# Latent attention: keys and queries stored by head, one score product per block of queries, rotary part padded to 128 rows

## The chip, the cores and the metric

The program runs on one core of one Trainium2 chip. The metric is the time in microseconds (us) that the device takes for one execution; lower is better. A core has a matrix engine (PE in the profile; PEld is its loading of the stationary operand), a vector engine (DVE), a scalar engine (ACT), GpSimd (POOL) and a queue engine (SP) that only issues transfers here.

## The reference

A two-layer decoder trunk over 512 tokens of width 1024. Every layer is a half-step feed-forward network, a token mixer, a second half-step feed-forward network and a gated embedding. Layer 0's mixer is a gated one; layer 1's mixer is the latent attention that the change touches:

```python
def mla_mixer(h, positions, w_in, q_a_norm, kv_a_norm, w_q_b, w_kv_b, q_norm, k_norm, w_out):
    z = h @ w_in
    c_q, c_kv, k_rope = jnp.split(z, [Q_LORA, Q_LORA + KV_LORA], axis=-1)
    q = (rms_norm(c_q, q_a_norm) @ w_q_b).reshape(bsz, seq, C_HEADS, C_QK)      # 8 heads, 128 + 64
    kv = (rms_norm(c_kv, kv_a_norm) @ w_kv_b).reshape(bsz, seq, C_HEADS, C_NOPE + C_V)
    k_nope, v = jnp.split(kv, [C_NOPE], axis=-1)
    k = jnp.concatenate([k_nope, broadcast(k_rope)], axis=-1)
    q, k = rms_norm(q, q_norm), rms_norm(k, k_norm)
    # the last 64 features of q and k are rotated by the position
    ...
    def attend(args):                       # a block of 128 queries
        s = jnp.einsum('bhqd,bhkd->bhqk', qb, k) * ATTN_SCALE
        s = jnp.where(key_pos <= q_pos, s, NEG_BIG)
        return jnp.einsum('bhqk,bhkd->bhqd', jax.nn.softmax(s), v)
    return out @ w_out
```

A score is thus a sum over 192 features: 128 plain ones of the head and 64 rotary ones.

## The kernel before, in words

All activations stand as tiles of 128 features by 512 tokens. Weight products are made from weights and inputs each cut into a high and a low part of a reduced float32 kind (`mm3`, lines 125 to 129; `mm3t`, lines 163 to 167): three products for each, with up to 512 columns. Inside the attention the operands are whole float32, and there a product that is not a transpose shows as two records in the trace.

`odd` (line 860) is the attention. `latent` makes the compressed keys, values and queries. `keys(c)` and `values(c)` each work on four heads, and leave keys by tokens; `turn_keys(c)` turns them to features by tokens. `queries(c)` works on two heads and is a generator: four steps make the queries of a block of 128 tokens each, then comes the rotation on POOL, then `turn` (line 1084) for each of the four blocks of tokens: two transposes for the heads' plain features, with a copy by ACT, and one for the two heads' rotary features, which lie in rows 0 to 63 and 64 to 127 of one tile, with a copy by DVE.

`score(h, i)` (line 1017) makes the scores of a head for the i-th block of 128 queries. As keys lie by blocks of tokens, it runs over the i + 1 blocks of keys and issues for each a product over 128 rows (line 1025) and a product over the head's 64 rotary rows (line 1026), each with 128 columns. Over 8 heads and 4 blocks these are 80 products of either kind. Then DVE adds the mask and takes the maximum, ACT takes the exponential, and DVE divides.

The order is that of the loop at line 1060 over 32 pairs (h, i), from which a scheduler makes a fixed order for each engine. A step transposes the scores (line 1067), has ACT copy them, takes one step of `fill` (the queries of the other heads) or of the output projection, issues the scores three pairs ahead, and multiplies by the values (line 1075). Scores and transposed scores take turns in four PSUM tiles named `pb`, so the scores of a pair go into the tile that the scores two pairs earlier leave when their exponential is done.

Of the kernel before, what the change touches and what calls it, by code (L numbers as in the profile page):

```python
# [29 lines left out]
# columns of the constants' array  # L30
C_ID, C_BASE, C_LEV, C_NEG, C_ONE, C_INV, C_END = 0, 128, 256, 576, 704, 705, 737
LEVELS = (4, 8, 16, 32, 64)
# columns of the small parameters' array
# [4 lines left out]
def turn_parts(shift):  # L38
    """2**shift / (2 pi), less whole turns, in three parts: of 12 bits after the point, of the next 12, and the rest;
    each over 2**shift"""  # L40
    from fractions import Fraction
    two_pi = Fraction(62831853071795864769252867665590057683943388, 10 ** 43)
    unit = Fraction(2) ** shift
    rest = unit / two_pi
    rest -= round(rest)
    parts = []
    for bits in (12, 24):
        part = Fraction(round(rest * 2 ** bits), 2 ** bits)
        parts.append(float(part / unit))
        rest -= part  # L50
    return parts + [float(rest / unit)]


class Net:
# [14 lines left out]
    def share(self, *engines):  # L69
        """who takes the weights' low parts, in turn"""  # L70
        self.cutters = cycle(engines or (self.nc.vector,))

# [24 lines left out]
    def weights(self, src, total, unit, keep=False, step=CW, eng=None):  # L97
        """(hi, lo, n) for each unit columns of src"""
# [14 lines left out]
    def cut(self, h, l, src, eng=None):  # L113
        """src (float32) into h + l"""
# [3 lines left out]
    def cut_scaled(self, h, l, src, g):  # L118
        """src * g, g a column, into h + l"""
# [11 lines left out]
    def feat(self, src, x):  # L131
        """[P features, T] = W.T x; src [P, nk * P], a column of tiles"""
# [9 lines left out]
    def feats(self, ws, x, pss, t):  # L142
        """several at a time, for the tokens t; a step is an input's tile. ws: for each the pieces of the weights"""
# [9 lines left out]
    def tok_steps(self, src, x, width, pss):  # L153
        """into pss, TB tiles [P tokens, width], x.T W; src [P, nk * width], k-major; a step is a k"""
# [14 lines left out]
    def tok_blocks(self, src, x, width):  # L169
        """for each block of tokens [P tokens, width] = x.T W, with all of W held"""  # L170
# [16 lines left out]
    def rsqrt_steps(self, v, n):  # L187
# [8 lines left out]
        # with h = v y^2: y (15 - 10 h + 3 h^2) / 8, here without a factor of 3 / 8  # L196
# [6 lines left out]
        # y (3 - v y^2) / 2, with that factor  # L203
# [6 lines left out]
    def sums(self, sqs):  # L210
        """[P tokens, TB * len(sqs)] sums over partitions of [P, T] tiles"""
# [7 lines left out]
    def spread(self, r, c0):  # L219
        """PSUM [P, T], each partition with the tokens' values r[:, c0:c0 + TB]"""  # L220
# [6 lines left out]
    def norm_of(self, acc, d):  # L227
        """the tokens' 1 / rms, a column per block"""
# [5 lines left out]
    def along(self, r):  # L234
        """the same along the free axis, in each partition"""
# [14 lines left out]
    def done(self, k, t=slice(0, T), later=False):  # L250
        """x[k] is final for the tokens t: its part of the next stage's input"""
# [7 lines left out]
    def add_sq(self, acc, src, first, last):  # L259
        """acc, the squares' sum"""  # L260
# [10 lines left out]
    def ffn(self, i, f, g_next, embedding=False, tail=None, first=None):  # L271
        """tail: what is left of the stage before, for the second half of the tokens, in steps"""
# [58 lines left out]
    def project_out(self, w, mixed, g_next, early):  # L331
        """mixed: a list that grows; the first three outputs' sums over its first early tiles run ahead, a step each"""
# [25 lines left out]
    def ple(self, i, g_next):  # L358
        """By halves of the tokens, so that the norm of one runs beside the products of the other; returns the steps
        left for the second half. Two tiles of outputs lie side by side."""  # L360
# [49 lines left out]
        def finish(half, m, pps):  # L410
            """the last two outputs, one by one; the squares' sum then is in the first half of its tile"""
# [72 lines left out]
        # the other half begins with the weights that the first ended with  # L484
# [10 lines left out]
    def even(self, j, g_next):  # L495
# [3 lines left out]
        # lower bounds: softmax over one row, its running sum less its first  # L499
# [117 lines left out]
        def advance(us):  # L617
            """the recurrence's steps, in turn by heads, beside so much of the projections"""
# [53 lines left out]
    def hgrn_head(self, f, k, q, v, h, outs):  # L672
        """Decay products instead of exponentials of sums of logarithms: every factor of a pair (s, t) is a product
        of gates after s up to t, cut at a block's boundary, but in blocks of four, which are cut in their middle,
        where a factor may be the inverse of two gates (no gate is under F_MIN)."""
# [36 lines left out]
        # inside blocks of four  # L712
# [8 lines left out]
        # from a block's left half to its right half; each pair belongs to one level  # L721
        tt = t4
        for li, b in enumerate(LEVELS):
# [12 lines left out]
            # blocks twice as long  # L736
# [10 lines left out]
        # the state before each block of 128 tokens but the first  # L747
# [33 lines left out]
    def rope_tables(self):  # L781
        """cos and sin of the positions' angles, [P tokens, TB * 32]"""
# [13 lines left out]
        # in turns: the angle is cut into three parts of 12 bits and a rest, whose products with a turn's parts are exact  # L796
        part, cnt, frac, turns, low = (self.small() for _ in range(5))

        def whole(out, src, scale, unit):
            """src * scale, rounded to multiples of the unit"""  # L800
# [27 lines left out]
        # cos(a) = sin(pi / 2 - |a|)  # L828
# [4 lines left out]
        # with the rope parts' gains: first half and second half  # L833
# [10 lines left out]
    def rotate(self, V, out, src, nm, nh):  # L844
        """out, src [P, TB, nh, 64]"""
# [14 lines left out]
    def odd(self, j, g_next):  # L860
# [7 lines left out]
        def latent(m0, n, col):  # L868
            """gained by features, and the squares' sum"""
# [11 lines left out]
        # the rotary key, by features and then by tokens  # L881
# [9 lines left out]
        # the factors of both norms, by tokens, and their squares: latent keys and values, latent queries  # L891
# [31 lines left out]
        # keys by four heads: [features, head, token] for each block of tokens  # L923
        kT, krT = [[None] * 2 for _ in range(TB)], [[None] * 2 for _ in range(TB)]
# [33 lines left out]
        def turn_keys(c):  # L958
            kn, krs = ks.pop(c)
            for tb in range(TB):  # L960
                if c == 0:
                    t = self.big()
                    krT[tb] = [t[:, :256], t[:, 256:]]
                kT[tb][c] = self.big()
                self.turn(kT[tb][c], krT[tb][c], kn[tb], krs[tb], par[:, S_KN:S_KN + 1])
# [9 lines left out]
        def queries(c):  # L975
            """of two heads; their factors of the norms go to the softmax"""
# [22 lines left out]
            qT = [[None, None] for _ in range(TB)]  # L999
            two = [self.big() for _ in range(2)]  # L1000
            rope = self.big()
            for tb in range(TB):
                qT[tb][0] = two[tb // 2][:, tb % 2 * 256:tb % 2 * 256 + 256]
                qT[tb][1] = rope[:, tb * P:(tb + 1) * P]
                self.turn(*qT[tb], qn[tb], qo[:, tb * P:(tb + 1) * P], par[:, S_QN:S_QN + 1])
                rq = next(steps, rq)
                if tb == 1:
                    yield True
# [5 lines left out]
            heads[c] = qT, rq, nq  # L1014

        # a head's scores for a block of queries, and the softmax
        def score(h, i):
            c4, e4, e2 = h // 4, h % 4, h % 2
            pair, po = e4 // 2, 64 * e2
            qT, rq, nq = heads[h // 2]  # L1020
            n = (i + 1) * P
            ps = self.pb()
            for jj in range(i + 1):
                u = slice(jj * P, (jj + 1) * P)
# [215 lines left out]
```

## Time and profile before

| what | value |
|---|---|
| median of 3 runs | 2084.04 us (2083.5 to 2087.65) |
| span of the profiled execution | 2083.4 us |
| PE busy | 2034.7 us, 98% of the span |
| DVE, ACT, POOL busy | 1062.0, 772.9, 163.1 us |
| mean granted clock of PE | 0.990 |

The page gives the profiled execution's span and no other time of it; 2083.4 us is 0.64 us below the median of the runs. A row of the timeline that ends in "x2" stands for two instructions in a row, and the length that it shows goes from the start of the first to the end of the last; as instructions overlap, the pace is read from the distance between starts.

### The profile page before, as it was taken

The numbers are of one execution on the slowest core, as the hardware profiler recorded it, in microseconds if no ns is written. First come the engines' busy times: TensorE is split into PE (matmuls) and PEld (weight loads), VectorE is DVE, ScalarE is ACT, GpSimd is POOL, SyncE is SP. The second block draws the span as 40 slices with busy tenths as digits, with TensorE's granted clock in tenths as the row PEclk, the third lists the DMA queues.
The fourth block names the chain that finished last, engine by engine and source line by source line (L and its number), as shares of the span: only waits on it lengthen the run. The fifth ranks groups of instructions, "written<-read, shape, count | busy, mean of one in ns | idle before, by whom it ended". The sixth has DMA issues, their size and how long they took to land.

```text
span 2083.4 us, 25822 instructions
## 1 busy us (share of the span) xinstructions
PE 2034.7 (98%) x9924; PEld 1708.6 (82%) x9924; DVE 1062.0 (51%) x2021; ACT 772.9 (37%) x1364; POOL 163.1 (8%) x152
## 2 busy tenths in 40 slices
PE   8999999999999999999899999999999999999997
PEld 6888888778888888889888888887778888888896
DVE  6444444676555444445874443445664554444456
ACT  5333333223343333334543333335543443333344
POOL 1000000210010000000210000003310100000002
PEclk9999999999999999999999999999999999999998
DMA  5333233222223232333422333332100232323333
GB/s 176 92 101 97 91 95 102 76 86 61 72 81 111 92 102 92 102 102 119 137 82 92 101 94 91 103 92 71 36 31 21 81 110 93 101 92 102 102 119 107
DMA packets 59324, 193.28 MB, mean 93 GB/s; under 512 B 6720, under 2 KB 9280, under 8 KB 59200
## 3 DMA queue, kind: packets, MB, share of 16 engines
q1 hardware_dynamic: 59200, 191.62, 29.7%
q8 instruction: 78, 1.28, 0.3%
q14 instruction: 46, 0.38, 0.1%
HBM read 189.50 MB, written 2.10 MB: 92 GB/s over the span
## 4 chain that ended last, share of the span: by engine, by line
PE 92%; DVE 5%; ACT 1%; DMA 1%; issue 0%; POOL 0%; SPq 0%; ACTq 0%; DVEq 0%; POOLq 0%
PE ps L127 26%; PE ps L129 26%; PE ps L128 26%; PE pb L1026 2%; PE pb L1025 1%; PE ps L165 1%; PE ps L166 1%; PE ps L167 1%; PE ps L1075 1%; DVE wl L116 1%; PE pb L730 1%; DVE big L693 1%; PE pb L129 1%; PE pb L128 1%; PE pb L127 1%; DMA raw<-in_w_gu 1%
## 5 line engine op out<-in xcount | busy, mean ns | idle before, releaser
L127 PE MATMUL ps<-big,wh 128*128 128x512 f32 (+1 forms) x2528 | 967.7, 383 | 9.1 <-ACT wh L115 5.9
L129 PE MATMUL ps<-big,wl 128*128 128x512 f32 (+1 forms) x2528 | 965.8, 382 | 8.3 <-DVE wl L116 8.2
L128 PE MATMUL ps<-big,wh 128*128 128x512 f32 (+1 forms) x2528 | 964.9, 382 | 0.0
L115 ACT CAST wh<-raw 128x512 fp32r<-128x512 f32 (+1 forms) x709 | 430.4, 609 | 1032.9 <-PE ps L128 857.0
L116 DVE TENSOR_TENSOR wl<-raw,wh 128x512 fp32r<-128x512 f32 (+1 forms) x677 | 486.0, 720 | 566.1 <-ACT wh L115 545.8
L129 PEld LDWEIGHTS ps<-big,wl 128*128 128x128 f32 x2528 | 475.8, 188 | 102.0 <-DVE wl L116 10.0
L127 PEld LDWEIGHTS ps<-big,wh 128*128 128x128 f32 x2528 | 475.8, 188 | 100.4 <-ACT wh L115 5.9
L128 PEld LDWEIGHTS ps<-big,wh 128*128 128x128 f32 x2528 | 476.1, 188 | 91.5 <-DVE big L116 0.2
L268 POOL TENSOR_TENSOR acc<-acc,tmp 128x512 f32<-128x512 f32 (+1 forms) x54 | 67.5, 1250 | 1587.9 <-ACT tmp L266 1587.0
L282 DVE TENSOR_TENSOR tmp<-ps,tmp 128x512 f32<-128x512 f32 x84 | 58.0, 691 | 117.4 <-PE ps L129 115.7
L280 DVE TENSOR_TENSOR tmp<-ps,rb 128x512 f32<-128x512 f32 x84 | 58.0, 691 | 115.7 <-PE ps L129 115.7
L121 DVE SCALAR_TENSOR_TENSOR big<-x,par,big 128x512 fp32r<-128x512 f32 (+1 forms) x72 | 58.2, 813 | 35.0 <-ACT big L120 34.5
L116 DVE TENSOR_TENSOR big<-tmp,big 128x512 fp32r<-128x512 f32 x96 | 67.7, 707 | 7.9 <-ACT big L115 1.1
L120 ACT ACTIVATE big<-x,par 128x512 fp32r<-128x512 f32 (+1 forms) x72 | 48.4, 673 | 60.8 <-DVE x L328 46.0
L115 ACT CAST big<-tmp 128x512 fp32r<-128x512 f32 x96 | 59.4, 620 | 27.8 <-DVE tmp L282 22.7
L281 ACT ACTIVATE tmp<-tmp 128x512 f32<-128x512 f32 x88 | 55.0, 631 | 23.4 <-DVE tmp L280 23.4
L165 PE MATMUL ps<-wh,big 128*128 128x512 f32 (+1 forms) x144 | 57.0, 396 | 1.4 <-ACT big L970 1.2
L166 PE MATMUL ps<-wl,big 128*128 128x512 f32 (+1 forms) x144 | 54.9, 382 | 2.5 <-DVE wl L116 2.5
L167 PE MATMUL ps<-wh,big 128*128 128x512 f32 (+1 forms) x144 | 55.1, 383 | 0.0
L116 POOL TENSOR_TENSOR wl<-raw,wh 128x512 fp32r<-128x512 f32 (+1 forms) x32 | 39.0, 1226 | 117.1 <-ACT wh L115 109.1
L1035 ACT ACTIVATE big<-pb,ty,ty 128x128 f32<-128x128 f32 (+3 forms) x32 | 19.8, 619 | 58.2 <-DVE ty L866 32.8
L1025 PE MATMUL pb<-big,big 128*128 128x128 f32 x160 | 36.0, 307 | 4.6 <-ACT big L1035 4.6
(234 smaller groups left out, 1417.9 us busy)
## 6 DMA issues: line engine op xcount, KB each, us to landing
raw<-in_w_gu SPq DMA_DIRECT2D x164, 512.0 KB, 3.5
raw<-in_w_dn SPq DMA_DIRECT2D x64, 512.0 KB, 3.5
raw<-in_w_pg SPq DMA_DIRECT2D x28, 512.0 KB, 3.5
raw<-in_w_dn SPq DMA_DIRECT2D x32, 384.0 KB, 3.1
raw<-in_w_ei SPq DMA_DIRECT2D x24, 512.0 KB, 3.6
raw<-in_w_gu SPq DMA_DIRECT2D x24, 256.0 KB, 2.6
raw<-in_w_eo SPq DMA_DIRECT2D x8, 512.0 KB, 3.5
raw<-in_w_mo SPq DMA_DIRECT2D x8, 512.0 KB, 3.7
```

The lines of the kernel that those rows point to most:

```text
L115: self.nc.scalar.copy(out=h, in_=src)
L116: (eng or self.nc.vector).tensor_tensor(out=l, in0=src, in1=h.bitcast(F32), op=ALU.subtract)
L121: self.nc.vector.scalar_tensor_tensor(out=l, in0=src, scalar=g, in1=h.bitcast(F32), op0=ALU.mult, op1=ALU.subtract)
L127: mm(ps, wh, xh, start=first, stop=False)
L128: mm(ps, wh, xl, start=False, stop=False)
L129: mm(ps, wl, xh, start=False, stop=last)
L165: mm(o, x[0][:, t], wh, start=first, stop=False)
L166: mm(o, x[0][:, t], wl, start=False, stop=False)
L167: mm(o, x[1][:, t], wh, start=False, stop=last)
L268: eng.tensor_tensor(out=acc, in0=acc, in1=sq, op=ALU.add)
L280: nc.vector.tensor_tensor(out=t, in0=gps, in1=rb, op=ALU.mult)
L282: nc.vector.tensor_tensor(out=t, in0=ups, in1=t, op=ALU.mult)
```

## The change

Keys are kept by head over all 512 tokens (`kT[h]`), and rotary keys by pairs of heads (`krT[h // 2]`, one head in rows 0 to 63, the other in rows 64 to 127). `turn` goes away: four transposes fill one PSUM tile of 512 columns, and one copy takes it out. Each pair of heads gets two padded rotary query tiles of 128 rows by 512 tokens: for one head rows 64 to 127 are zero, for the other rows 0 to 63. POOL writes the zeros once for two sets of tiles, which the four pairs of heads use in turn. `score` then issues two products, each over 128 rows and with all (i + 1) * 128 columns.

```diff
-        kT, krT = [[None] * 2 for _ in range(TB)], [[None] * 2 for _ in range(TB)]
+        kT, krT = [None] * 8, [None] * 4
...
         def turn_keys(c):
             kn, krs = ks.pop(c)
-            for tb in range(TB):
-                if c == 0:
-                    t = self.big()
-                    krT[tb] = [t[:, :256], t[:, 256:]]
-                kT[tb][c] = self.big()
-                self.turn(kT[tb][c], krT[tb][c], kn[tb], krs[tb], par[:, S_KN:S_KN + 1])
+            for e in range(4):
+                ps = self.ps()
+                for tb in range(TB):
+                    nc.tensor.transpose(out=ps[:, tb * P:(tb + 1) * P], in_=kn[tb][:, e * P:(e + 1) * P], identity=self.ident)
+                kT[4 * c + e] = self.big()
+                S.activation(out=kT[4 * c + e], in_=ps, func=AF.Copy, scale=par[:, S_KN:S_KN + 1])
+            for e in range(2):
+                ps = self.ps()
+                for tb in range(TB):
+                    nc.tensor.transpose(out=ps[:, tb * P:(tb + 1) * P], in_=krs[tb][:, e * P:(e + 1) * P], identity=self.ident)
+                krT[2 * c + e] = self.big()
+                V.tensor_copy(out=krT[2 * c + e], in_=ps)
...
-            qT = [[None, None] for _ in range(TB)]
-            two = [self.big() for _ in range(2)]
-            rope = self.big()
+            qT, qz = [self.big() for _ in range(2)], pads[c % 2]
+            for e in range(2):
+                ps = self.ps()
+                for tb in range(TB):
+                    nc.tensor.transpose(out=ps[:, tb * P:(tb + 1) * P], in_=qn[tb][:, e * P:(e + 1) * P], identity=self.ident)
+                S.activation(out=qT[e], in_=ps, func=AF.Copy, scale=par[:, S_QN:S_QN + 1])
+                rq = next(steps, rq)
+                rq = next(steps, rq)
+                if e == 0:
+                    yield True
+            ps = self.ps()
             for tb in range(TB):
-                qT[tb][0] = two[tb // 2][:, tb % 2 * 256:tb % 2 * 256 + 256]
-                qT[tb][1] = rope[:, tb * P:(tb + 1) * P]
-                self.turn(*qT[tb], qn[tb], qo[:, tb * P:(tb + 1) * P], par[:, S_QN:S_QN + 1])
-                rq = next(steps, rq)
-                if tb == 1:
-                    yield True
+                nc.tensor.transpose(out=ps[:, tb * P:(tb + 1) * P], in_=qo[:, tb * P:(tb + 1) * P], identity=self.ident)
+            for e in range(2):
+                u = slice(64 * e, 64 * e + 64)
+                V.tensor_copy(out=qz[e][u, :], in_=ps[u, :])
...
             ps = self.pb()
-            for jj in range(i + 1):
-                u = slice(jj * P, (jj + 1) * P)
-                nc.tensor.matmul(ps[:, u], qT[i][0][:, e2 * P:(e2 + 1) * P], kT[jj][c4][:, e4 * P:(e4 + 1) * P], start=True, stop=False)
-                nc.tensor.matmul(
-                    ps[:, u], qT[i][1][po:po + 64, :], krT[jj][c4][po:po + 64, pair * P:(pair + 1) * P], start=False, stop=True)
+            nc.tensor.matmul(ps[:, :n], qT[e2][:, t], kT[h][:, :n], start=True, stop=False)
+            nc.tensor.matmul(ps[:, :n], qz[e2][:, t], krT[h // 2][:, :n], start=False, stop=True)
...
+        pads = [[self.big() for _ in range(2)] for _ in range(2)]
+        for two in pads:
+            for e in range(2):
+                G.memset(two[e][64 - 64 * e:128 - 64 * e, :], 0.0)
         keys(0)
```

**On PE, the scores of head 3 for its last block of queries.** Before, in line 1025's and line 1026's products (`pb` is the scores' tile; the operands behind the arrow are a key tile and a query tile):

```order
L1025 MATMUL pb_12578<-big_11700,big_12036 128x128 [waits PE_49]
L1026 MATMUL pb_12578<-big_11699,big_12037 128x128
L1025 MATMUL pb_12578<-big_11712,big_12036 128x128
L1026 MATMUL pb_12578<-big_11711,big_12037 128x128
L1025 MATMUL pb_12578<-big_11724,big_12036 128x128
L1026 MATMUL pb_12578<-big_11723,big_12037 128x128
L1025 MATMUL pb_12578<-big_11736,big_12036 128x128
L1026 MATMUL pb_12578<-big_11735,big_12037 128x128
```

After the change the same scores are two rows; line 1036 has the plain and line 1037 the rotary features. Of the rows that follow, line 1080 transposes an earlier block of scores, line 1036 begins the next head's first block, line 1088 multiplies by values, and lines 1037 and 1009 are that block's rotary part and the turning of the last queries:

```order
L1036 MATMUL pb_12506<-big_11733,big_12014 128x512
L1037 MATMUL pb_12506<-big_11747,big_11309 128x512
L1080 MATMUL pb_12519<-cst,big_12429 128x128 [waits DVE_49,PE_49]
L1080 MATMUL pb_12519<-cst,big_12429 128x128
L1036 MATMUL pb_12534<-big_11754,big_12288 128x128 [waits Activation_49]
L1088 MATMUL ps_12482<-big_12485,big_11438 128x128 [waits Activation_49]
L1037 MATMUL pb_12534<-big_11782,big_11306 128x128
L1080 MATMUL pb_12548<-cst,big_12470 128x128 [waits DVE_49]
L1080 MATMUL pb_12548<-cst,big_12470 128x128 x2
```

Eight products of 128 columns have become two of 512, and none of the new ones has fewer than 128 rows.

**On PE, where the queries of heads 2 and 3 are turned** (line 1091 before, lines 1009 and 1017 after; `ps` tiles hold the transposes). Before:

```order
L1091 MATMUL ps_12038<-cst,big_11910 128x128
L1025 MATMUL pb_12062<-big_11700,big_11791 128x128 [waits Activation_49]
L1026 MATMUL pb_12062<-big_11699,big_11793 128x128
L1075 MATMUL ps_11957<-big_12003,big_11430 128x128 [waits Activation_49]
L1075 MATMUL ps_11957<-big_12003,big_11439 128x128
L1091 MATMUL ps_12042<-cst,big_11883 128x128 [waits Pool_49]
```

After:

```order
L1009 MATMUL ps_12053<-cst,big_11956 128x128
L1036 MATMUL pb_12031<-big_11719,big_11792 128x256 [waits Activation_49]
L1088 MATMUL ps_11941<-big_11981,big_11438 128x128 [waits Activation_49]
L1088 MATMUL ps_11941<-big_11981,big_11447 128x128
L1037 MATMUL pb_12031<-big_11740,big_11307 128x256
```

The scores for block 1 of head 1 still stand behind a wait for ACT, and the transposes of the rotary queries, which wait for POOL, have moved from before them to behind two more groups of line 1088.

**On POOL, between the weights for `values(0)` and for `keys(1)`** four writes of zeros stand now:

```order
L116 TENSOR_TENSOR wl_11428<-raw_11421,wh_11423 128x512 [waits DVE_49,PE_49,Activation_49]
L1052 MEMSET big_11306 64x512 [waits Pool_49]
L1052 MEMSET big_11307 64x512
L1052 MEMSET big_11308 64x512
L1052 MEMSET big_11309 64x512
L116 TENSOR_TENSOR wl_11472<-raw_11469,wh_11471 128x512 [waits DVE_49,PE_49,DMAHW6_49,Activation_49,Pool_49]
```

They are new; the rows around them are in the order that they had.

## Rows read from the trace of the kernel before

**Rows 1.** The page, busy us of each engine with its share of the span.
```profile
PE 2034.7 (98%) x9924; PEld 1708.6 (82%) x9924; DVE 1062.0 (51%) x2021; ACT 772.9 (37%) x1364; POOL 163.1 (8%) x152
```

**Rows 2.** Stretches of the attention: length, busy us by engine, PEclk, DMA share, GB/s.
```profile
1490.00:1510.00 20.00, 18.49 (x96) 15.65 (x96) 10.96 (x45) 7.92 (x21) 3.72 (x6) 0.83 0.09 29
1570.00:1616.00 46.00, 46.00 (x262) 36.60 (x262) 19.83 (x59) 15.29 (x41) 0.00 (x0) 1.00 0.08 24
1476.00:1616.00 140.00, 135.22 (x765) 111.11 (x765) 76.28 (x278) 58.31 (x153) 16.74 (x22) 0.96 0.09 27
```

**Rows 3.** Groups by line, 1440 to 1620: shapes, count | busy, mean ns | idle before.
```profile
L1026 PE MATMUL pb<-big,big 64*128 64x128 f32 x160 | 39.6, 328 | 0.0
L1025 PE MATMUL pb<-big,big 128*128 128x128 f32 x160 | 36.0, 307 | 4.6 <-ACT big L1035 4.6
```

**Rows 4.** PE timeline, head 6's blocks 1 to 3, head 7's block 0: start, length, what.
```profile
1582.42 0.38 PE L1025 MATMUL pb<-big,big 128*128 128x128 f32 x2
...
1583.98 0.94 PE L1075 MATMUL ps<-big,big 128*128 128x128 f32 x6
...
1585.19 0.39 PE L1025 MATMUL pb<-big,big 128*128 128x128 f32 x2
...
1587.59 1.16 PE L1075 MATMUL ps<-big,big 128*128 128x128 f32 x8
1588.58 0.27 PE L1067 MATMUL pb<-cst,big 128*128 128x128 f32 x1
...
1591.45 0.38 PE L1025 MATMUL pb<-big,big 128*128 128x128 f32 x2
...
1594.67 0.49 PE L1075 MATMUL ps<-big,big 128*128 128x128 f32 x2
1595.00 0.38 PE L1067 MATMUL pb<-cst,big 128*128 128x128 f32 x2
1595.22 0.39 PE L1025 MATMUL pb<-big,big 128*128 128x128 f32 x2
...
1595.95 0.55 PE L1067 MATMUL pb<-cst,big 128*128 128x128 f32 x3
1596.25 0.48 PE L127 MATMUL ps<-big,wh 128*128 128x512 f32 x1
...
1597.49 0.45 PE L1025 MATMUL pb<-big,big 128*128 128x128 f32 x2
```

**Rows 5.** PE timeline elsewhere: float32 products of 64 and 128 columns, reduced ones of 512.
```profile
503.85 1.89 PE L730 MATMUL pb<-big,big 128*128 128x64 f32 x16
...
506.31 0.39 PE L772 MATMUL pb<-big,big 128*128 128x128 f32 x2
506.53 0.39 PE L774 MATMUL pb<-big,big 128*128 128x128 f32 x2
...
950.52 0.39 PE L127 MATMUL ps<-big,wh 128*128 128x512 f32 x1
950.75 0.39 PE L128 MATMUL ps<-big,wh 128*128 128x512 f32 x1
```

**Rows 6.** The softmax of head 6's last block on DVE (mask) and ACT (exponential).
```profile
1594.78 0.30 DVE L1029 TENSOR_TENSOR pb<-pb,cst 128x128 f32<-128x128 f32 x1 [2.02 <-PE pb L1026]
...
1596.53 0.78 ACT L1035 ACTIVATE big<-pb,ty,ty 128x512 f32<-128x512 f32 x1 [4.50 <-PE pb L1067]
```

**Rows 7.** PE timeline: the two longest waits of the stage.
```profile
1493.39 0.49 PE L1025 MATMUL pb<-big,big 128*128 128x128 f32 x2 [1.51 <-ACT big L1035]
...
1550.48 0.49 PE L1025 MATMUL pb<-big,big 128*128 128x128 f32 x2 [2.30 <-ACT big L1035]
```

**Rows 8.** Copies out of the turning, by line: ACT and DVE before, and POOL's gap.
```profile
L1095 ACT ACTIVATE big<-ps,par 128x256 f32<-128x256 f32 x16 | 7.2, 480 | 2.5 <-PE ps L1091 2.5
L1095 ACT ACTIVATE big<-ps,par 128x512 f32<-128x512 f32 x8 | 5.3, 687 | 1.7 <-PE ps L1091 1.6
1445.68 3.67 POOL L866 TENSOR_TENSOR big<-big,ty 128x256 f32<-128x256 f32 x4 [3.66 <-DVE ty L207]
```

More of the change, by code (lines that the diff above doesn't have):

```diff
@@ L1013, in queries @@
             V.tensor_scalar(out=nq, in0=rq, scalar1=-1.0, scalar2=None, op0=ALU.mult)
-            heads[c] = qT, rq, nq
+            heads[c] = qT, qz, rq, nq
         def score(h, i):
-            c4, e4, e2 = h // 4, h % 4, h % 2
-            pair, po = e4 // 2, 64 * e2
-            qT, rq, nq = heads[h // 2]
+            e2 = h % 2
+            qT, qz, rq, nq = heads[h // 2]
             n = (i + 1) * P
+            t = slice(i * P, n)
             ps = self.pb()
-            for jj in range(i + 1):
-                u = slice(jj * P, (jj + 1) * P)
-                nc.tensor.matmul(ps[:, u], qT[i][0][:, e2 * P:(e2 + 1) * P], kT[jj][c4][:, e4 * P:(e4 + 1) * P], start=True, stop=False)
-                nc.tensor.matmul(
-                    ps[:, u], qT[i][1][po:po + 64, :], krT[jj][c4][po:po + 64, pair * P:(pair + 1) * P], start=False, stop=True)
-            t = slice(i * P, n)
+            nc.tensor.matmul(ps[:, :n], qT[e2][:, t], kT[h][:, :n], start=True, stop=False)
+            nc.tensor.matmul(ps[:, :n], qz[e2][:, t], krT[h // 2][:, :n], start=False, stop=True)
             V.tensor_tensor(out=ps[:, t], in0=ps[:, t], in1=self.cst[:, C_NEG:C_NEG + P], op=ALU.add)
@@ L1082, in odd @@
             pass
-    def turn(self, main, rope, mp, rp, g):
-        nc = self.nc
-        for o, s, scale in ((main, mp, g), (rope, rp, None)):
-            n = o.shape[1]
-            ps = self.ps()
-            for e in range(0, n, P):
-                nc.tensor.transpose(out=ps[:, e:e + P], in_=s[:, e:e + P], identity=self.ident)
-            if scale is None:
-                nc.vector.tensor_copy(out=o, in_=ps[:, :n])
-            else:
-                nc.scalar.activation(out=o, in_=ps[:, :n], func=AF.Copy, scale=scale)
     def run(self):
```

## The prediction
> **What bounds the kernel now.** I read the page's engine line first, to see which engine has no slack. PE is busy for 98% of the span and DVE, the next, for 51% [rows 1], so work taken from PE shortens the time unless another engine is late. Next the stretches of the attention, since only they change. From 1476 to 1616 PE works for 135.22 of 140.00 us and waits for 4.78; DVE works for 76.28 and ACT for 58.31; from 1570 on PE waits for nothing [rows 2]. The groups by line then show what of this is scores: 160 records each on lines 1025 and 1026, two for each of 80 products [rows 3]. Their busy times overlap, so the timeline gives the price, from start to start.
>
> In head 6 the scores of block 1 stand from 1582.42 to 1583.98, of block 2 from 1585.19 to 1587.59 and of block 3 from 1591.45 to 1594.67; head 7's block 0 takes 1595.22 to 1595.95 [rows 4]. That is 1.56, 2.40, 3.22 and 0.73 us, 7.91 us a head for 40 records, 0.198 each. Elsewhere two records of 128 columns over 128 rows take 0.22 us, 0.11 each, and sixteen of 64 columns take (1.89 - 0.27) / 15 = 0.108 each, 0.27 being the length of one record [rows 4, 5]. So the alternation of 128-row and 64-row products costs nearly twice what a stream of 128-row ones does, and from 64 to 128 columns almost nothing is added: there the loading of 128 stationary columns sets the pace, not the columns.
>
> **The change part by part.**
>
> *Scores, before.* 8 heads x 7.91 = 63.3 us. What follows a 64-row product also starts late: eight records of line 1075 take 0.99 us where 8 x 0.11 = 0.88, two take 0.33 where 0.22; behind block 0 nothing is lost [rows 4]. I count 0.11 behind three of four blocks, 24 x 0.11 = 2.6. Sum 65.9 us.
>
> *Scores, after.* 32 blocks x 2 products x 2 records = 128 records. The columns stay the same in number: 320 times 128. No row of the trace has a float32 product of over 128 columns. From above: in proportion to 128 columns, 320 x 0.11 = 35.2 us; or each record as two goes of the reduced kind, whose 512 columns start 0.23 us apart [rows 5], so 0.46 for 512 columns and 320 x 0.115 = 36.8. From below: each record as one go, 0.23, 0.17 and 0.115 us for 512, 384 and 256 columns and the floor of 0.108 for 128: 0.623 x 4 records x 8 heads = 20 us. I take 36, by the row of the same kind of product, since the one-go price belongs to another kind. The Trainium skill, "FP8 and Floating Point Precision", TensorE Precision Notes, gives true float32 four passes through the array, which in two records would be 36.8 us; no run here shows it. Gain 65.9 - 36 = 30 us, at the bounds 29 and 46.
>
> *The padding.* 64 more rows of zeros add no columns. 64-row products do not take less now than 128-row ones, 39.6 us against 36.0 for equal counts [rows 3]. I cost it at 0, and its gain is in the term above.
>
> *The turning.* The transposes stay 96 in number. ACT's copies were 8 x 0.687 + 16 x 0.480 = 13.2 us and become 16 of 512 columns, 11.0 us [rows 8]. DVE's 24 copies become 12 of 512 columns, 8 of them over half the rows. Their price is not in the rows; by ACT's 0.687 they take 8.2 us, and DVE is idle for 64 of 140 us [rows 2]. Where it counts is the end of the turning, where the first rotary scores wait for two such copies, 1.4 us, in place of one small one. The three plain products that now come first cover some of it. Between 0 and +1.4 I take +1.
>
> *POOL's zeros.* Four writes of 64x512. The nearest row is four products of 128x256, 3.67 us, and POOL had idled for 3.66 just before them [rows 8]. At twice the columns the writes could take up to 7.3 us, in the same gaps between weights, and behind them the low parts of the weights for `keys(1)` wait, and PE for those. 0 to +3.6; I take 0, as a write of zeros reads nothing. If the gap closes, the wait shows on line 166.
>
> *The waits.* With shorter scores the softmax has less cover. A head's second block needs the `pb` tile of the last block of the head before. From that block's end to the second block's start 2.82 us passed [rows 4]: the mask starts at 1594.78 and the exponential ends at 1596.53 + 0.78 = 1597.31 [rows 6]. In it PE had 0.33 + 0.22 + 0.73 + 0.30 us of its own and 1.24 of the output projection [rows 4]. After, its own part is 0.22 + 0.22 + 0.44 + 0.33 = 1.2 us, so up to 1.6 us is open wherever the order puts nothing else there. The built order puts the turning of queries there for two heads, where the waits of 1.51 and 2.30 us stand already [rows 7], and query blocks or output projection for the rest. I keep the waits that are there and add 0.5 us at four places: +2.
>
> *Sum.* -30 + 1 + 0 + 2 = -27. Against the span of 2083.4 us that is 2056.4. The median of the runs lies 0.64 us above this span, so I forecast **2057.0**. DVE, at 76 us in what becomes a stretch of some 113, is next in line but not the bound. What comes after the stage waits for PE and moves up with it.
>
> **The rivals.**
>
> *Softmax bound, 2067.8.* The open 1.6 us is paid at all 8 heads: -30 + 1 + 12.8 = -16.2. For it: DVE also carries the queries' work for the first heads, and 2.30 us were lost there already [rows 7]. Against it: in the late heads DVE idled 2.02 us before a mask, waiting for PE [rows 6].
>
> *Loads not hidden, 2071.* Each of the 128 records pays its load before its columns: 128 x 0.108 = 13.8 more, so -30 + 13.8 + 3 = -13.2. Against it: records of 128 rows, each with a load of its own, start 0.11 us apart, where load and columns in turn would give 0.198 as in the alternation [rows 4, 5]. The Trainium skill, "TensorE: Matmul & The Clock Gate", Part 3, What overlaps and what doesn't, says that a weight load overlaps a running matmul only when the row groups differ. By that rule the padding would give this time and take away the one thing that lets the 64-row loads overlap; the trace does not agree, 0.11 us with equal rows and 0.198 with different ones.
>
> *Cheap columns, 2047.* Scores at their lower bound of 20 us. The softmax then takes some back: -46 + 1 + 8 = -37.
>
> *The clock falls, slower, 2091.6.* After the wait of 1.51 us the granted clock over 1490 to 1510 is 0.83 [rows 2, 7]. With the two levels of 1.2 and 2.4 GHz that is 6.8 us at the lower one, and 3.4 us lost. If all 8 heads wait 1.6 us and seven more drop so: -30 + 1 + 12.8 + 23.8 = +7.6. It decides from five more drops on, where -30 + 1 + 12.8 + 17 = +0.8. Against it: from 1570 to 1616 the clock stays at 1.00 [rows 2], and the built order leaves few such places.
>
> *No effect, 2083.* If a long product runs as four short ones at 0.198 us each, only the 2.6 us behind the blocks would go, and the waits take them back. Against it: nothing of 128 rows runs so slowly at full clock.
>
> **How the numbers follow.** Forecast 0.70, softmax 0.13, loads 0.05, cheap columns 0.04, clock 0.05, no effect 0.03. The forecast's own range is 2048 (the 4.78 us of waits go as well, no cost of turning, scores at 35.2) to 2064 (zeros at +3.6, waits at +5). With the softmax case it reaches 2069, and 2048 to 2069 then holds some 0.80. A measurement of this kernel can tell about 0.2% from no change, 4.2 us. Faster by more: 0.70 + 0.13 + 0.05 + 0.04 = 0.92; within: 0.03; slower: 0.05.
>
> **What would show it.** The new score lines should have 64 records each, those of 512 columns some 0.44 us apart when nothing else stops them; a head's scores take 4.5 us for 7.91. PE's wait in the stage should be 5 to 9 us, on line 1036 for ACT. If 512 columns start 0.55 us apart, the loads are not hidden; at 0.23, columns are cheap. If PE waits over 15 us in the stage, the softmax is the bound; a granted clock below 0.90 over the stage would be the slower case. The forecast is wrong if the stage shortens by under 20 us or over 35.

## The result and the profile after

The changed kernel takes **2057.8 us** (median of 4 runs, 2056.87 to 2060.5) against 2085.34 us of the kernel before in the same series (4 runs, 2083.5 to 2087.65): a ratio of **0.9865**, 95% interval 0.9851 to 0.9879, or 27.5 us less. The forecast was 2057.0 in a range of 2048 to 2069. The profiled execution of the changed kernel is the slowest of its four, 2060.5 us with a span of 2058.8.

The engine line of the page, which answers to [rows 1]: busy us, share of the span, instructions.

```profile
PE 2008.0 (98%) x9732; PEld 1686.2 (82%) x9732; DVE 1063.9 (52%) x2009; ACT 770.5 (37%) x1356; POOL 164.8 (8%) x156
```

PE lost 26.7 us of work and 192 records, and is the bound as before. The other engines do what they did.

The stretches of the attention in the changed kernel, with the columns of [rows 2]. The last row goes from the first score to the last group of products with the values:

```profile
1490.00:1510.00 20.00, 17.71 (x105) 14.48 (x104) 15.37 (x58) 10.68 (x28) 6.92 (x9) 1.00 0.17 53
1570.00:1616.00 46.00, 46.00 (x225) 36.59 (x224) 28.79 (x55) 21.99 (x46) 7.14 (x5) 1.00 0.16 52
1481.14:1589.04 107.90, 101.59 (x565) 81.81 (x563) 77.71 (x273) 56.50 (x147) 16.64 (x22) 0.98 0.11 35
```

The same stretch, from first score to last group of values, in the kernel before:

```profile
1474.75:1613.85 139.10, 134.31 (x760) 110.20 (x758) 76.76 (x282) 58.79 (x155) 16.74 (x22) 0.96 0.09 27
```

This stretch went from 139.1 to 107.9 us, 31.2 less. What follows it is unchanged: 2083.4 - 1613.85 = 469.6 us before and 2058.8 - 1589.04 = 469.8 after. What precedes it is 6.4 us longer. Of that, 3.8 us were there before the first keys, in code that is the same (the reduction of line 216 just ahead of them starts at 1428.95 before and at 1432.72 after); a second execution, below, shows that they belong to the one execution. The rest lies between line 216 and the first score, and is taken up under the turning. So stretches are compared here, and spans only by medians.

PE's timeline of the changed kernel, with the columns of [rows 4], shows a block of 384 columns, and later one of 512 followed by the next head's block of 128:

```profile
1500.49 0.81 PE L1036 MATMUL pb<-big,big 128*128 128x384 f32 x2
1501.13 0.81 PE L1037 MATMUL pb<-big,big 128*128 128x384 f32 x2
1501.78 0.50 PE L1088 MATMUL ps<-big,big 128*128 128x128 f32 x3
...
1558.41 1.02 PE L1036 MATMUL pb<-big,big 128*128 128x512 f32 x2
1559.26 1.02 PE L1037 MATMUL pb<-big,big 128*128 128x512 f32 x2
1560.12 0.38 PE L1088 MATMUL ps<-big,big 128*128 128x128 f32 x2
1560.34 0.38 PE L1080 MATMUL pb<-cst,big 128*128 128x128 f32 x2
1560.56 0.39 PE L1036 MATMUL pb<-big,big 128*128 128x128 f32 x2
1560.78 0.39 PE L1037 MATMUL pb<-big,big 128*128 128x128 f32 x2
1561.01 0.49 PE L1080 MATMUL pb<-cst,big 128*128 128x128 f32 x3
```

From start to start, a product of two records takes 0.855 us with 512 columns, 0.645 with 384 and 0.22 with 128, so a record of 512 columns takes 0.43. Blocks of 256 columns take 0.43 a product (the one on line 1037 that starts at 1496.89 is followed at 1497.32). A head's scores are 2 x (0.855 + 0.645 + 0.43 + 0.22) = 4.3 us, and eight heads 34.4, where the prediction had 63.3 from [rows 4], and 65.9 with what followed late. Nothing follows late now: two records of line 1088 take 0.22 behind the scores.

The groups by line from 1440 to 1600 in the changed kernel, with the columns of [rows 3]: 64 records a line, a mean that contains the overlap, and the idle time before them.

```profile
L1036 PE MATMUL pb<-big,big 128*128 128x512 f32 x16 | 8.3, 598 | 1.4 <-ACT big L1044 1.4
L1037 PE MATMUL pb<-big,big 128*128 128x512 f32 x16 | 8.2, 592 | 0.0
L1036 PE MATMUL pb<-big,big 128*128 128x256 f32 x16 | 5.4, 418 | 4.0 <-ACT big L1044 4.0
```

PE's waits in the changed kernel from 1475.6 to 1592, which is the end of the turning and the whole stretch: us in total, times, longest.

```profile
PE pb L1036 <- ACT big L1044: 5.4, 3, 2.1
PE ps L963 <- DVE big L971: 1.2, 1, 1.2
PE ps L1088 <- ACT big L1082: 0.5, 1, 0.5
PE ps L1017 <- DVE big L116: 0.2, 1, 0.2
```

The scores still wait for the softmax at three places, 5.4 us for 4.6 before [rows 3], and most of it at second blocks, those of 256 columns. New is a wait in the turning, at line 963, for DVE's copies of 512 columns (line 971).

### The profile page after: what moved, and what is told of

It reads as the page before. It is cut to its first block, busy times and chain, and to the rows that moved or that the text cites. A ratio compares the mean times of both kernels' runs of the same rounds, so it can differ in the third digit from the quotient of the medians.

```text
span 2058.8 us, 25411 instructions
## 1 busy us (share of the span) xinstructions
PE 2008.0 (98%) x9732; PEld 1686.2 (82%) x9732; DVE 1063.9 (52%) x2009; ACT 770.5 (37%) x1356; POOL 164.8 (8%) x156
## 4 chain that ended last, share of the span: by engine, by line
PE 90%; DVE 6%; ACT 2%; DMA 1%; issue 1%; POOL 0%; SPq 0%; DVEq 0%; ACTq 0%; POOLq 0%
PE ps L127 27%; PE ps L129 26%; PE ps L128 26%; PE ps L165 1%; PE ps L166 1%; PE ps L167 1%; PE pb L730 1%; PE pb L129 1%; DVE wl L116 1%; PE pb L128 1%; DVE big L693 1%; PE pb L127 1%; PE ps L1088 1%; PE pb L216 1%; PE pb L1036 0%
## 5 line engine op out<-in xcount | busy, mean ns | idle before, releaser
L120 ACT ACTIVATE big<-x,par 128x512 fp32r<-128x512 f32 (+1 forms) x72 | 48.4, 673 | 61.5 <-DVE x L328 45.9
L115 ACT CAST big<-tmp 128x512 fp32r<-128x512 f32 x96 | 59.4, 620 | 28.4 <-DVE tmp L282 22.7
L129 PE MATMUL pb<-big,wl 128*128 128x256 f32 (+1 forms) x112 | 37.3, 333 | 2.3 <-DVE wl L116 2.3
L127 PE MATMUL pb<-big,wh 128*128 128x256 f32 (+1 forms) x112 | 37.5, 335 | 0.0
```

Source lines behind the costliest of these rows:

```text
L115: self.nc.scalar.copy(out=h, in_=src)
L127: mm(ps, wh, xh, start=first, stop=False)
L129: mm(ps, wl, xh, start=False, stop=last)
```

## The experiments

My theory after the result: PE paid for every change between products of 128 and of 64 rows, and the change takes these away; the longer products and the padding itself do nothing else. Rivals: the gain is in the smaller number of products; or the order by head, not the padding, gives it; or the loads are not hidden and other things made up for it.

### Long products without the zeros

```diff
-            nc.tensor.matmul(ps[:, :n], qz[e2][:, t], krT[h // 2][:, :n], start=False, stop=True)
+            u = slice(64 * e2, 64 * e2 + 64)
+            nc.tensor.matmul(ps[:, :n], qz[u, t], krT[h // 2][u, :n], start=False, stop=True)
```

One copy of 128 rows takes the rotary queries out, and POOL's zeros go.

> Keys and queries by head and long products as in the changed kernel, but the rotary products run over the head's 64 rows, with no zeros. Theory (the gain is that no product of another row count stands between, so that loads are hidden again): a record beside one of other row count pays its load of about 0.09 us before its columns, as it did before (0.198 against 0.11). 128 records x 0.09 = 11.5 us, and some 2 us behind the blocks: about 2071, 13 us over the changed kernel; two records of 512 columns start 0.52 us apart in place of 0.43. Rival (the gain is that there are 128 records in place of 320): no slower than the changed kernel by more than 1 us, 2058.

Measured: 2061.69 us (2061.01 to 2063.38), ratio 0.9891 (0.9874 to 0.9908). PE's timeline of this kernel:

```profile
1544.54 1.02 PE L1034 MATMUL pb<-big,big 128*128 128x512 f32 x2
1545.50 1.12 PE L1036 MATMUL pb<-big,big 64*128 64x512 f32 x2
1546.55 0.49 PE L1084 MATMUL ps<-big,big 128*128 128x128 f32 x2
1546.87 0.38 PE L1076 MATMUL pb<-cst,big 128*128 128x128 f32 x2
```

The block of 512 columns takes 2.01 us for 1.72 (four records of 0.43), and the two records behind it 0.32 for 0.22: 0.39 more for two changes of the row count, 0.195 each.

PE's loads (PEld) in this block and, below them, the load of the first padded record in the change's block of 512 columns:

```profile
1544.43 0.30 PEld L1034 LDWEIGHTS pb<-big,big 128*128 128x128 f32 x2
1545.49 0.29 PEld L1036 LDWEIGHTS pb<-big,big 64*128 64x128 f32 x2 [0.76 <-issue]
```
```profile
1558.84 0.19 PEld L1037 LDWEIGHTS pb<-big,big 128*128 128x128 f32 x1 [0.24 <-issue]
```

In the change this load starts 0.42 us ahead of its product (1559.26) and is over in 0.19. Without the zeros no load ran for 0.76 us, and yet the 64-row load starts only 0.01 us ahead of the row of its product (1545.50). So at a change of the row count the load is not hidden behind the product ahead of it; why it is held back, the traces do not say.

The work is there as the theory has it, but of the 13 us that I had expected the time shows 3.9: 2061.69 against the change's 2057.8. That was settled with the runs side by side, below.

### The padding with short products

```diff
-            nc.tensor.matmul(ps[:, :n], qT[e2][:, t], kT[h][:, :n], start=True, stop=False)
-            nc.tensor.matmul(ps[:, :n], qz[e2][:, t], krT[h // 2][:, :n], start=False, stop=True)
+            for jj in range(i + 1):
+                u = slice(jj * P, (jj + 1) * P)
+                nc.tensor.matmul(ps[:, u], qT[e2][:, t], kT[h][:, u], start=True, stop=False)
+                nc.tensor.matmul(ps[:, u], qz[e2][:, t], krT[h // 2][:, u], start=False, stop=True)
```

> The changed kernel with its zeros, but each score product cut into pieces of 128 columns, 160 products in the order that the kernel before had. Theory: 320 records x 0.11 = 35.2 us where the long ones took 34.5: 2058 to 2059, the whole gain is still there. Rival (the gain is in fewer records): 320 records at up to 0.198, about 2085; if each half has half of the gain, about 2071.

Measured: 2059.73 us (2058.34 to 2061.48), ratio 0.9881 (0.9866 to 0.9896). The first and the last of the 16 records of a block of 512 columns, and what follows, in PE's timeline:

```profile
1558.17 0.39 PE L1038 MATMUL pb<-big,big 128*128 128x128 f32 x2
...
1559.73 0.39 PE L1039 MATMUL pb<-big,big 128*128 128x128 f32 x2
1559.96 0.39 PE L1090 MATMUL ps<-big,big 128*128 128x128 f32 x2
```

Sixteen records take 1.79 us, 0.11 each, though every one loads its own 128 columns; four records of 512 columns take 1.71. So the smaller number of products is worth 0.08 us a block here, and the equal rows the rest of 3.22 - 1.71.

### Fewer changes of the row count in the old layout

```diff
-                nc.tensor.matmul(ps[:, u], qT[i][0][:, e2 * P:(e2 + 1) * P], kT[jj][c4][:, e4 * P:(e4 + 1) * P], start=True, stop=False)
...
+                one, two = (plain, rope) if jj % 2 == 0 else (rope, plain)
+                nc.tensor.matmul(ps[:, u], *one, start=True, stop=False)
+                nc.tensor.matmul(ps[:, u], *two, start=False, stop=True)
```

This is the kernel before, with plain and rotary products in the order P R R P P R R P.

> The kernel before, but for every second block of keys the rotary product comes first, so that two products of 64 rows, then two of 128 rows stand side by side, and rows change half as often. Theory in the form that the change of rows costs, some 0.09 us for each of the two records on its either side: half of the 31 us is saved, about 2070. Theory in the form that 64-row records are slow by themselves: the time of the kernel before, 2085, or the 128-row half alone gets faster, about 2077.

Measured: 2077.29 us (2073.68 to 2078.75), ratio 0.9964 (0.995 to 0.9977). A block of four keys in PE's timeline:

```profile
1569.75 0.38 PE L1028 MATMUL pb<-big,big 128*128 128x128 f32 x2
1570.06 0.48 PE L1029 MATMUL pb<-big,big 64*128 64x128 f32 x2
1570.38 0.38 PE L1028 MATMUL pb<-big,big 64*128 64x128 f32 x2
1570.70 0.49 PE L1029 MATMUL pb<-big,big 128*128 128x128 f32 x2
...
1572.30 0.39 PE L1077 MATMUL ps<-big,big 128*128 128x128 f32 x2
```

The block takes 2.55 us for 3.22 with the same products in another order. I had expected more because I had counted half of the changes as gone; the built order has 110 of them for 160. With 50 x 0.195 = 9.8 us fewer, the stretch from first score to last values took 130.0 us for 139.1, and the time fell by 8.2. The other theory on record, that 64-row products are slow by themselves, allowed 2077 as well, and the time met it; the rows decide against it. The 64-row pair at 1570.38, which follows another of 64 rows, is 0.38 us long, as a 128-row pair among its like is (0.39 at 1572.30), and the longer pairs, 0.48 and 0.49, stand behind a change in either direction. So the alternation itself is what costs, without padding, long products or another layout.

### No rotary part in the scores

```diff
-            nc.tensor.matmul(ps[:, :n], qT[e2][:, t], kT[h][:, :n], start=True, stop=False)
-            nc.tensor.matmul(ps[:, :n], qz[e2][:, t], krT[h // 2][:, :n], start=False, stop=True)
+            nc.tensor.matmul(ps[:, :n], qT[e2][:, t], kT[h][:, :n], start=True, stop=True)
```

> The changed kernel without the rotary product of the scores (that part of the score is left out). PE has 17.3 us less to do in the stage. If PE is still the bound: about 2042, with waits of PE as now. If the softmax is close behind, as the rival had it, the waits grow at the second block of each head and at the turning of queries: 8 x 0.7 = 6 us and more given back, 2047 to 2052.

Measured: 2051.73 us (2048.86 to 2052.47), ratio 0.9839 (0.9824 to 0.9855). PE has 17 us less to do (half of 34.4) and gains 6. The two longest entries of PE's waits between first score and last values:

```profile
PE pb L1036 <- ACT big L1043: 10.7, 6, 2.4
PE ps L1087 <- ACT big L1081: 1.7, 5, 0.9
```

The waits for the softmax double, from 5.4 to 10.7 us. All of PE's idle time in the stretch goes from 6.3 to 14.0 us, and its granted clock is 0.95 for 0.98, so of the 17 us some 8 go to waits and some 3 to the clock. So the softmax stands close behind: what is still taken from the scores now pays about a third.

### Where the other work stands

```diff
-        for _ in range(3):
+        for _ in range(2):
             next(fill)
```

The number of pieces of the queries' work done before the first values was 3; tried were 2, 4 and 5.

> The changed kernel with two steps of the queries of heads 2 and 3 ahead of the loop in place of three, so that the turning of queries comes one pair later and a block of queries stands where PE waited for 1.81 and 2.15 us. If those waits are the order's doing: 2 to 5 us less, 2053 to 2056. If DVE's queue makes them wherever the turning stands: no change within 2 us.

> The same with four steps ahead, so that the turning comes one pair earlier, together with the first scores. Order's doing: the wait of 1.81 us stays or moves to the rotary queries that wait for POOL, the one of 2.15 us goes: 0 to 3 us less. DVE's queue: no change within 2 us.

> The same with five steps ahead: all four blocks of queries of heads 2 and 3 stand before the first transposed scores, and the turning of heads 6 and 7 comes two pairs earlier. Order's doing: 1 to 4 us less, since one turning leaves the head's end; against it, less work is left for the later waits. DVE's queue: no change within 2 us.

Measured: 2057.45 us with two (2055.71 to 2060.95; ratio 0.9867, 0.985 to 0.9885), 2059.9 with four (0.9875, 0.986 to 0.989), 2061.55 with five (0.9884, 0.9869 to 0.9898). With two, the scores' waits for the softmax are 3.8 us in five pieces for 5.4 in three; with four a wait for POOL's rotation comes in, in PE's waits:

```profile
PE pb L1036 <- ACT big L1044: 4.7, 4, 2.2
PE ps L1017 <- POOL big L858: 2.9, 1, 2.9
```

With five, the wait for POOL is 3.6 us and those for the softmax are 6.5. Against the change, none of it shows a gain that a measurement can tell.

### Four kernels side by side

> The changed kernel once more, on one chip with the three others of this group, so that they can be set against each other. Its first measurement gave 2057.8 us against 2085.3, and that profile had two things that the kernels beside it did not have: it reached the reduction of line 216 at 1432.7 us, where the others stood there between 1428.9 and 1431.9, and it took 36.1 us from there to the first transposes of the keys, where all the others took 34.5. If these belong to that one execution and not to the change, the profile of this run has 34.5 us there, the attention again takes some 108 us from the first score to the last group of values, and the median is 2056 to 2059 us. If they belong to the change, 36 us stands there again.

> Long products by head, but rotary products of 64 rows and no zeros, once more, beside the change on the same chip. If each change between 128-row and 64-row products costs PE 0.195 us, PE has some 11 to 12 us more to do than with the padding. What shows in the time is less where PE waits for the softmax in any case: those waits were 5.4 us with the padding and 3.7 us without. My theory of partly hidden work gives 3 to 6 us more than the change. If the padding did nothing, the difference is under 1.5 us; if nothing were hidden it is 11 to 12.

> The padding with products of 128 columns, once more, beside the change. If the gain is the equal rows and not the smaller number of products, its time is within 2 us of the change (its first measurement was 1.9 us above on another chip); if each of the 192 records that it has more than the change cost something of its own, 0.05 us each would make it 10 us slower.

> The change with two in place of three pieces of other work pulled ahead of the first values, once more, beside the change. Its first measurement, on another chip than the change, was 2057.45 us, and its waits for the softmax were 3.8 in place of 5.4 us. If that is worth anything, its median lies 1 to 2 us below the change's in the same group; if the waits are only moved, the two agree within 1 us.

| kernel, beside 2086.19 us of before | median (range), us | ratio (95% interval) | changes of row count | first score to last values, us |
|---|---|---|---|---|
| the change | 2058.09 (2055.66 to 2059.29) | 0.9873 (0.9856 to 0.9891) | 0 | 106.72 |
| long products, no zeros | 2063.39 (2062.95 to 2066.55) | 0.99 (0.9884 to 0.9916) | 60 | 113.98 |
| zeros, short products | 2060.15 (2059.51 to 2061.89) | 0.9883 (0.9867 to 0.9898) | 0 | 110.50 |
| the change with two pieces | 2056.21 (2053.08 to 2057.43) | 0.986 (0.9844 to 0.9876) | 0 | 106.85 |

In the change's second profile the reduction of line 216 stands at 1429.03, and 34.5 us lie between it and the first transposes of the keys: the late start in the first profile was that execution's. The stretch of the attention is 106.7 us, at a granted clock of 1.00.

The zeros are worth 5.3 us by the medians, and the ranges lie apart. The other 22.8 us of the change's 28.1 come without any zeros: long products by head leave 60 of the 160 changes. With the zeros, short products have nearly the whole gain too. The same stretch in the kernel without them and, below it, in the change:

```profile
1481.20:1595.18 113.98, 110.26 (x564) 79.89 (x563) 75.40 (x269) 56.68 (x147) 16.65 (x22) 0.99 0.11 33
```
```profile
1477.26:1583.98 106.72, 100.39 (x565) 80.36 (x563) 77.12 (x273) 56.42 (x147) 16.65 (x22) 1.00 0.11 35
```

PE has 9.9 us more work without the zeros (60 x 0.195 = 11.7 by the price of a change) but waits 3.7 us for 6.3, so the stretch is 7.3 us longer. The longer scores cover part of the softmax. These two profiles are the slowest of four runs and the fastest of four. Like with like is the first profile of the kernel without zeros, whose stretch had a granted clock of 1.00 as the change's has here: 112.3 us, 5.6 longer, which fits the 5.3 of the medians. The short products cost 2.1 us, and the ranges lie apart, but the granted clock was 0.97 in their stretch where the change had 1.00. The first profiles of both, at 0.98 each, lie 1.5 us apart (109.4 and 107.9 us), about what the paces give: 320 records at 1.79 / 16 are 35.8 us for 34.4. So some 1.4 us are likely their own. The changes of the row count are counted in the built order of PE. The kernel with two pieces has the lower median here by 1.9 us, and by 0.4 in the two first measurements, but the ranges overlap.

### The copies in the turning

The turning had cost more than my sum had for it. PE's timeline of the change's second profile, in the turning of the keys:

```profile
1468.93 1.24 PE L963 MATMUL ps<-cst,big 128*128 128x128 f32 x8
1472.48 1.09 PE L963 MATMUL ps<-cst,big 128*128 128x128 f32 x8 [2.31 <-DVE big L971]
```

DVE's timeline there, where lines 866 to 197 scale the first queries:

```profile
1468.16 0.65 DVE L866 TENSOR_TENSOR ty<-ty,ty 128x8 f32<-128x8 f32 x1
...
1470.23 0.92 DVE L193 TENSOR_SCALAR ty<-ty 128x8 int32<-128x8 int32 x1
1471.19 0.64 DVE L197 TENSOR_TENSOR ty<-ty 128x8 f32<-128x8 f32 x1
1471.75 1.28 DVE L971 COPY big<-ps 128x512 f32<-128x512 f32 x2
...
1474.13 0.17 DVE L866 TENSOR_TENSOR ty<-ty,ty 128x8 f32<-128x8 f32 x1
```

One of POOL's rows beside the operation of line 193:

```profile
1470.12 1.01 POOL L116 TENSOR_TENSOR wl<-raw,wh 128x384 fp32r<-128x384 f32 x1
```

The two copies stand behind five small operations that take 0.64 to 0.92 us each, and the PSUM tiles that PE wants come free with them. Each of the five ends about 0.03 us after one of POOL's operations does, that of line 193 at 1471.15 after POOL's at 1471.13. In the kernel before, the copies stood singly between the steps of the same chain. So one pair of copies was moved to ACT, in the kernel with two pieces:

```diff
-                V.tensor_copy(out=krT[2 * c + e], in_=ps)
+                (S.copy if c == 0 else V.tensor_copy)(out=krT[2 * c + e], in_=ps)
```

> The kernel with two pieces pulled ahead, and in the turning the two copies of rotary keys for the first four heads on ACT and not on DVE. In the change PE waited 2.3 us in the turning for these copies, since they stand on DVE behind the chain that scales the first queries, whose steps took 0.64 to 0.92 us each there; from the first transposes of the keys to the first score 13.7 us passed, where 11.3 passed before the change. If that wait is the part of the turning that my sum missed, it shrinks to under 0.8 us and the first score comes 11.5 to 12.7 us after the first transposes; the time then is 2054 to 2056 us, some 1.5 us below the kernel with two pieces (2056.2 and 2057.5 us in two measurements), which a measurement can hardly tell. If ACT is the next to be late, since it has four copies of its own there, PE waits as long for line 965 or 1010 and 13.7 us stand again.

Measured: **2054.61 us** (5 runs, 2052.9 to 2058.12) beside 2087.44 of before, ratio 0.9846 (0.9833 to 0.986). PE's timeline of this kernel at the same place:

```profile
1475.37 2.25 PE L963 MATMUL ps<-cst,big 128*128 128x128 f32 x16
1477.46 1.04 PE L969 MATMUL ps<-cst,big 128*128 128x128 f32 x8
```

The sixteen transposes that a wait had split now run in one piece, and all that is left for DVE is 0.45 us later, at line 1017. From the first transposes to the first score 11.3 us pass. This execution came late to the attention (line 216 at 1432.99), as the change's first one did, which took 12.35 us there; like with like, 1.0 us is gained. It is the lowest median of the study; its interval still overlaps the change's, so that it beats the change is likely and not shown.

## Why the prediction was right

**Scores, -30.** Measured 34.4 - 65.9 = -31.5. The value taken, two columns' time for each float32 column, held: 0.43 us for a record of 512 columns, where 0.44 was foretold and 0.23 was the cheap end. The other end of the step, which the loads set, held as well: with equal rows a load stays hidden at 128 columns (0.11 us a record) and at 512, where it starts 0.42 us ahead of its product.

By the Trainium skill's page "FP8 and Floating Point Precision", TensorE Precision Notes, a true float32 product makes four passes; 0.855 us for two records, beside four times the 0.23 of [rows 5], agrees with that within 0.07 us.

**Why the alternation cost.** The prediction said that it cost, from [rows 4, 5]; the runs give its price. Over a block of four keys, each change of the row count costs (3.22 + 0.11 - 1.79) / 8 = 0.19 us in the kernel before, where 0.11 is the late start behind the block, (2.55 - 1.79) / 4 = 0.19 in the mixed order, and 0.195 without zeros. And 160 x 0.195 = 31.2 is nearly the gain of the scores, 31.5. The rival of loads not hidden (2071) is out: it had records of 512 columns 0.55 us apart, and they start 0.43 apart.

The Trainium skill's page "TensorE: Matmul & The Clock Gate", Part 3, What overlaps and what doesn't, has loads overlap a running matmul only between different row groups. The runs do not agree: 0.11 us a record, with the load hidden, where the rows are equal, and 0.19 us on top wherever products of 128 rows and of 64 of these rows take turns. None of the experiments sets products of disjoint rows side by side.

**The padding, 0, and POOL's zeros, 0.** Right. POOL's timeline in the changed kernel:

```profile
1429.29 2.21 POOL L1052 MEMSET big<- 64x512 f32 x4
1433.49 1.26 POOL L116 TENSOR_TENSOR wl<-raw,wh 128x512 fp32r<-128x512 f32 x1 [1.99 <-ACT wh L115]
```

Four writes take 2.2 us, where the bound was 7.3, and the low part of the weights behind them waits for ACT another 1.99 us.

**The turning, +1.** This term was mis-sized, and its upper end of +1.4 too: from line 216 to the first score 45.8 us passed before, and 48.4 and 48.2 in the two profiles of the change, +2.4 to +2.6. In the first profile 1.6 of this lies ahead of the first transposes, at a granted clock of 0.91 for 0.95; from the first transposes to the first score it took 12.35 us for 11.3. The second took 13.7 there, and with it nine of the eleven profiles that have these copies on DVE, so +2.4 is the size of the term. The step that failed took the last two copies as the place where it counts. The place was in the middle: two copies of 512 columns behind DVE's chain, for whose PSUM tiles PE waited 1.2 and 2.3 us. Moving them to ACT brought 1.0 back, in an execution that came late as the first one did; what it brings in the others is not shown.

**The waits, +2.** Idle time of PE between first score and last values went from 4.8 to 6.3 us, +1.5, and 5.4 of it on line 1036 for ACT, as the prediction said; the places are mostly second blocks, where the wait comes as the softmax of the head before ends. The softmax rival (2067.8) needed over 15 us of waiting; the order had work for most heads. The run without the rotary part shows how near it was.

**The clock, not in the sum.** The sum took the clock as unchanged, and the rival had it falling. It rose: 0.96 over the stretch before, 0.98 and 1.00 in the two profiles after. At 0.96, 8% of 139.1 us lie at the lower of the two levels, and at 0.98, 4% of 107.9, which is 11.1 against 4.3 us, of which half is lost where PE has work: up to 3.4 us of gain. The first 20 us of [rows 2] show it, 0.83 before and 1.00 after. But the kernel before has one profile only, and over the whole program the granted clock averages 0.9897 over 30 runs of the kernel before and 0.9901 over the eight of the change, which is 21.6 against 20.3 us lost. So of the medians' 27.5 us the clock has about 1, and that the change raises it is not shown.

**The sum.** -31.5 + 1.5 is -30.0, and the stretch shortened by 31.2 (32.4 in the second profile); the rest fits the clock in these profiles. With +2.5 for the turning, -28.7 to -29.9 follows, and from line 216 to the end the profiles have 28.4 and 29.6 us less; the medians say 27.5 and 28.1. So 2057.0 against 2057.8 is right in its main term, and nearer than its small terms deserved: a turning too cheap by 1.5 us and a gain of scores and clock too small by some 3 lie on opposite sides.

## What to carry to other kernels

Read the pace of matmuls from start to start and compare it with a stream of equal ones: a pace that no column count explains pointed here to the change between row counts, which padding, but also a mere change of order (P R R P), takes away. Doubling the rows with zeros cost PE nothing: among their like, pairs of 64 and of 128 rows took the same 0.38 to 0.39 us. When copies are merged into fewer and longer ones, look at what stands ahead of them on their engine and who waits for their buffers, not only at the last of them.

## What the runs showed of the hardware that I had not expected

- A change between a product of 128 rows and one of 64 rows costs 0.19 us on average, with 128 columns and with 512 alike (0.39 for the two changes of a long block). Both directions cost about the same: by the rows of the mixed order, the first two records of 64 rows start 0.09 and 0.10 us late, and the first two of 128 rows behind them 0.10 and 0.10.
- DVE's copy of 64x512 takes 0.686 us and its copy of 128x512 0.68 (lines 1021 and 971): half the rows save nothing there either.
- DVE's operations on 128x8 took 0.64 to 0.92 us while POOL worked, and 0.15 to 0.17 from 1471.80 on, when POOL's last one had ended, in the change's second profile (line 866 shows both above). The Trainium skill's page "Trainium Architecture — The Big Picture", What this means for kernel authors, says that these two engines share a port pair by an exclusive lock; the rows fit it, as each of DVE's five long operations there ends just behind one of POOL's, but no run here moved POOL's work away.
